# A one-core decoder block: the projections' weight sums on VectorE instead of GpSimd, and rotary units with five tiles and earlier loads

## The chip, the core and the metric

One Trainium2 chip, one core of it. A core has TensorE (PE in the rows: matmuls), VectorE (DVE), ScalarE (ACT), GpSimd (POOL) and SyncE (SP, which here only issues loads), with an on-chip memory (SBUF), eight accumulator banks (PSUM) and DMA queues to the memory of the chip. An engine works through its instructions in the order in which they stand in its queue; an instruction whose input is missing holds up all that stands behind it. The metric is the device time of one execution in microseconds. Three executions of the kernel before took 1737.4, 1739.75 and 1740.69 us; the median, 1739.75 us, is the time before.

## The reference, cut to what matters

A block of a decoder on 1024 tokens of 1024 features in float32: one wide projection of the normed input feeds a recurrent branch (LRU) and a dilated-window attention branch; gates merge the two; a SwiGLU feed-forward layer follows.

```python
h = rms_norm(x, pre_mix_norm)
xr, gr, q, k, v, gates = split(h @ w_in)            # the projections
xr = causal_depthwise_conv(xr, conv_w, conv_b)      # 4 taps
xr = rg_lru(xr, ...)                                # two gate matmuls, then a scan over time
y_lru = (xr * gelu(gr)) @ w_lru_proj
q, k = partial_rope(q, cos, sin) * HEAD_DIM ** -0.5, partial_rope(k, cos, sin)   # 32 of 128 features
y_attn = dilated_window_attention(q, k, v) @ w_attn_proj
x = x + rms_norm((g_lru * y_lru + g_attn * y_attn) @ w_out)     # g_*: sigmoid(gates)
x = x + rms_norm((silu(n @ w_ffn_gate) * (n @ w_ffn_up)) @ w_ffn_down)           # n: rms_norm(x)
```

## The kernel before

The program runs in stages: the v projection (to about 140 us), the other projections (to about 720), attention with the LRU's and attention's output projections (to about 950), `w_out`, the feed-forward products (1060 to 1510) and the down projection. All but the middle stages are made of **quads**. A quad is a 2 by 2 block product done in seven block products instead of eight (Strassen's scheme in Winograd's form): `P1, P2, P6, P5, P3, P7, P4`, in this order on PE. A float32 operand is split into a high and a low part (`split`, L98 and L99: ACT writes the high part `whi`, DVE subtracts and writes the low part `wlo`), and a product is three matmuls, high-high, low-high and high-low (L133 to L135), for each of four blocks of 128 rows: 12 matmuls of 128x512 to a product, each product into one PSUM bank `pq`.

The projections stage has 28 quads: 0 to 7 for `gr` and `xr` in turn, 8 to 19 for q and k (three attention groups of four heads), 20 to 27 for the gates `gl` and `ga`. `Quad.prep` prepares the weights of a quad while PE is in the quad before it. It loads two blocks `r0` and `r1` (tiles `wraw`, two buffers, both on SP's queue), forms four sums of 128x512 each on GpSimd (L267 to L270: the two halves of `sb` and of `sa`), and splits `r0` (for P1 and P2), `sa` (P6 and P7), `sb` (P5 and P3) and half of `r1` (`w4h`, `w4l`, one buffer, for P4). `sa` and `sb` have one buffer each. As `wraw` has two buffers, the load of a next `r1` waits until the last split of this one, `w4l`, has read it. In `body`, DVE adds the finished products to each other: `uw` (L309), and `fb` (L728, in `proj`), which GpSimd's queue stores (L734).

After every product `run_quads` calls `tick()`, which runs what `todo` has for that count (7 to a quad). There are two kinds of extra work:

- 16 LRU units, from tick 15 on, one every 8 ticks. `lru_a` loads 515 columns of `xr`, forms the convolution on DVE in four instructions (L776, and three times L778: `xc`) and splits it (`xch`, `xcl`); `lru_b`, four ticks later, has six gate matmuls (`pgt<-xch,gw` and `pgt<-xcl,gw`), then sigmoids on ACT, a product on GpSimd (L799), a product and the scan on DVE (L800, L803), and a second product on GpSimd (L807).
- 6 rotary units, ticks 148 to 173, one every 5 ticks. `rotate_load` loads four tiles of 256 KB (`rq1`, `rq2` from the stored q and k, `rcs` and `rsn` from a table `rtd`), five ticks ahead of `rotate`, which has six products or sums on DVE (L825 to L830) and two stores on GpSimd's queue (L833).

Both kinds take their tiles from one ring of `B2` = 10 buffers (tag `b2`), so a load waits for the last reader of a buffer ten tiles earlier. The order of the instructions on an engine isn't the code's alone: where the program is built, instructions that don't depend on each other can be exchanged, as L269 ahead of L268 in some quads. The feed-forward quads use the same class later.

Of the kernel before, what the change touches and what calls it, by code (L numbers as in the profile page):

```python
# [40 lines left out]
EARLYP = {6: (0,), 7: (1,)}  # L41
ORDER = [(s[0], int(s[1])) for s in "t6 h1 p2 p3 x5 h0 t7 x6 x4 h2 x7 h3".split()]
B4 = 19
B2 = 10
LRU0, LRUD = 15, 8
ROPE0, ROPED = 148, 5


V_CB, V_BR, V_BI, V_LAM, V_CW, V_GP, V_END = 0, 8, 16, 24, 32, 64, 72
# [13 lines left out]
def block(ctx, tc, a, out):  # L63
    nc = tc.nc
    V, A, G, T = nc.vector, nc.scalar, nc.gpsimd, nc.tensor
# [19 lines left out]
    def b4(name, dt=F32, shape=(128, 1024)):  # L85
        return bp.tile(list(shape), dt, name=name, tag="b4")
# [7 lines left out]
    def split(src, hi, lo, he=None, le=None):  # L94
        if he is G:
            G.tensor_scalar(hi, src, 1.0, 0.0, op0=OP.mult, op1=OP.add)
        else:
            A.activation(hi, src, AF.Copy)  # L98
        (le or V).tensor_sub(lo, src, f(hi))  # L99
# [132 lines left out]

    class Quad:
        pool = up = X = None
        P1B, W4 = 2, 1
        NAMES = dict(P1="b11", P2="b21", P6="t2", P7="t3", P5="t1", P3="b22", P4="t4")
        w = None
# [22 lines left out]
            self.unit(self.raw(0, name), ("P1", "P2"))  # L260

        def prep(self):
            r0, r1 = self.raw(0), self.raw(1)
            lo_, hi_ = slice(0, 512), slice(512, 1024)
            sa = Quad.pool.tile([128, 1024], F32, name="sa")
            sb = Quad.pool.tile([128, 1024], F32, name="sb")
            G.tensor_add(sb[:, lo_], r1[:, lo_], r1[:, hi_])  # L267
            G.tensor_sub(sa[:, lo_], sb[:, lo_], r0[:, lo_])  # L268
            G.tensor_sub(sa[:, hi_], r0[:, lo_], r1[:, lo_])  # L269
            G.tensor_sub(sb[:, hi_], r0[:, hi_], sa[:, lo_])  # L270
            if self.w is None:
                self.w = {}
                self.unit(r0, ("P1", "P2"))
            self.unit(sa, ("P6", "P7"))
            self.unit(sb, ("P5", "P3"))
            h4 = Quad.pool.tile([128, 512], F32R, name="w4h", bufs=Quad.W4)
            l4 = Quad.pool.tile([128, 512], F32R, name="w4l")
            split(r1[:, hi_], h4, l4)
            self.w["P4"] = h4, l4
# [47 lines left out]
    def run_quads(quads, pre, tick=None):  # L327
        quads[0].prep()
        for j in range(pre):
            quads[j].first()  # L330
        for j, q in enumerate(quads):
            if j + 1 < len(quads):
                quads[j + 1].prep()
            for _ in q.body():
                if tick:
                    tick()
            if pre <= j + 1 < len(quads):
                quads[j + 1].head()
                if tick:
                    tick()  # L340
                quads[j + 1].first()
                if tick:
                    tick()
# [92 lines left out]
    def rates(ss):  # L436

        s = sp.tile([128, 4], F32, name="rs4", bufs=2)
        last_act[0] = A.activation(s, ss, AF.Sqrt, bias=epsc, scale=1.0 / D)
        r = sp.tile([128, 4], F32, name="rr4", bufs=2)  # L440
        V.reciprocal(r, s)
        e = sp.tile([128, 4], F32, name="re4", bufs=2)
        V.scalar_tensor_tensor(e, ss, D * EPS, r, op0=OP.add, op1=OP.mult)
        V.scalar_tensor_tensor(e, e, 1.0 / D, r, op0=OP.mult, op1=OP.mult)
        V.scalar_tensor_tensor(e, e, -3.0, r, op0=OP.add, op1=OP.mult)
        V.tensor_scalar(r, e, -0.5, None, op0=OP.mult)
        dg = sp.tile([128, 4, 128], F32, name="dg")
        for t in range(4):
            last_dve[0] = V.tensor_scalar(dg[:, t], ident, e[:, t:t + 1], None, op0=OP.mult)
        rb = ps("prb")  # L450
        last_rb[0] = T.matmul(rb, ones, dg.rearrange("p t n -> p (t n)"), start=True, stop=True)
        return r, rb
# [65 lines left out]
    r0, rb = rates(ss[0])  # L518
# [13 lines left out]
    r1, rb = rates(ss[1])  # L532
# [222 lines left out]
    def b2(name, dt=F32, shape=(128, 512)):  # L755
        return lp.tile(list(shape), dt, name=name, tag="b2")
# [64 lines left out]
    def rotate(g, u):  # L821

        t1, t2, cs, sn = RT.pop((g, u))
        m1, m2 = b2("rm1"), b2("rm2")
        V.tensor_mul(m1, t2, sn)  # L825
        V.tensor_mul(m2, t1, sn)
        V.tensor_mul(t1, t1, cs)
        V.tensor_mul(t2, t2, cs)
        V.tensor_sub(t1, t1, m1)
        V.tensor_add(t2, t2, m2)  # L830
        c = slice(512 * u, 512 * u + 512)
        for i, t in enumerate((t1, t2)):
            G.dma_start(qkd[g, :, :, 16 * i:16 * i + 16, c].rearrange("h s p n -> (h s) p n"), t)  # L833
# [5 lines left out]
    todo = {1: [(late_rates, ())]}  # L839
# [3 lines left out]
        todo.setdefault(LRU0 + LRUD * n, []).append((lru_a, unit))  # L843
        todo.setdefault(LRU0 + LRUD * n + 4, []).append((lru_b, unit))
    for n in range(6):
        todo.setdefault(ROPE0 + ROPED * (n - 1), []).append((rotate_load, (n // 2, n % 2)))
        todo.setdefault(ROPE0 + ROPED * n, []).append((rotate, (n // 2, n % 2)))
    clock = [0]

    def tick():  # L850
        clock[0] += 1
        for fn, args in todo.pop(clock[0], ()):
            fn(*args)
# [9 lines left out]
    ap = actx.enter_context(tc.tile_pool(name="ap", bufs=2, reuse_waits="tile"))  # L863
    lp = lctx.enter_context(tc.tile_pool(name="lp", bufs=B2, reuse_waits="tile"))
    op1 = fctx.enter_context(tc.tile_pool(name="op1", bufs=1, side="right", reuse_waits="tile"))
# [224 lines left out]
    for n, (fn, args) in enumerate(EARLYA):  # L1090
        todo.setdefault(fn, []).append((after, args))
    run_quads(q1, PRE1, tick)
    assert not todo
    fctx.close()
# [65 lines left out]
    for nb in range(KT):  # L1160
        if nb % 2 == 0:
            w = wunit(a["w_ap"][nb // 2])
        mx, m1 = b4("mix"), b4("m1")
# [110 lines left out]
    quads = [q for i in range(NF // 2) for q in hidden(i)]  # L1274
# [58 lines left out]
    octx = ExitStack()  # L1333
    op = octx.enter_context(tc.tile_pool(name="op", bufs=1, side="right", reuse_waits="tile"))
    Quad.up = op
    run_quads(quads, PRE)


# [146 lines left out]
    def fetch(n):  # L1485
        if n < len(steps):
            ops[steps[n]] = operands(*steps[n])
# [117 lines left out]
```

## Time and profile before

| what | value |
|---|---|
| median of three executions | 1739.75 us |
| the profiled execution | 1737.8 us |
| its span from the first to the last instruction | 1736.0 us |
| PE busy | 1676.3 us, 97% of the span |
| DVE, ACT, POOL busy | 1121.0, 728.4, 693.2 us |

The profiled execution took 1737.8 us, of which 1.8 us lie outside the span. A busy PE isn't always PE at its full rate: at the lower of its two clocks a matmul takes longer and counts as busy all the same. So in the rows further down the number of matmuls in a stretch and the column PEclk (the clock that was granted, as a share of the full one) are read beside the busy time. The rows name an instruction by its line, engine, operation and `out<-in`; numbers of buffers are left out where they don't matter. In a list of waits the columns are the total time, the number of times and the longest time; in a timeline, start, length and, in brackets, the idle time of the engine ahead of the instruction with what ended it.

### The profile page before, as it was taken

The page shows a single profiled execution, that of the slowest core. Times are in us where ns is not written, and L with a number is a line of the kernel's source. Part 1 is how long each engine was busy: PE and PEld are TensorE (multiplying, and loading weights), DVE is VectorE, ACT ScalarE, POOL GpSimd, SP SyncE. Part 2 cuts the span into 40 slices and gives each one's busy share as a digit, 9 for nine tenths or more (in the row PEclk, how much of TensorE's full clock was granted, in tenths as well). Part 3 has the DMA queues.
Part 4 walks back from the last instruction along what each step waited for, and adds up shares of the span by engine and source line. Part 5 has one row for each costly group of instructions (what it writes and reads, how often), then busy time and mean ns, then how long its engine had stood idle before and what let it go on. Part 6 is the DMA issues. An engine that isn't in the chain of part 4 may idle for free.

```text
span 1736.0 us, 21088 instructions
## 1 busy us (share of the span) xinstructions
PE 1676.3 (97%) x7748; PEld 1376.8 (79%) x7748; DVE 1121.0 (65%) x1591; ACT 728.4 (42%) x1130; POOL 693.2 (40%) x644
## 2 busy tenths in 40 slices
PE   9999999999999999989999999799999999999996
PEld 7897888787877887868888787678888888788885
DVE  7956577778887766554433678755554555659658
ACT  6423367564555532564441445323222222345343
POOL 2003454554445533133334205576566666400103
PEclk9999999999999999999999999899999999999998
DMA  8233433343333564683519742133222222475353
GB/s 322 85 123 123 146 128 130 131 149 118 128 133 134 167 206 156 229 317 135 195 50 359 245 147 73 61 123 126 103 91 103 92 96 105 160 255 191 109 188 121
DMA packets 95919, 262.70 MB, mean 151 GB/s; under 512 B 13768, under 2 KB 22120, under 8 KB 94408
## 3 DMA queue, kind: packets, MB, share of 16 engines
q1 hardware_dynamic: 70352, 182.49, 31.2%
q0 software_dynamic: 20352, 76.21, 11.6%
q10 hardware_dynamic: 5112, 2.66, 0.5%
q8 instruction: 61, 1.00, 0.2%
q14 instruction: 42, 0.34, 0.1%
HBM read 180.86 MB, written 80.35 MB: 150 GB/s over the span
## 4 chain that ended last, share of the span: by engine, by line
PE 77%; DVE 10%; DMA 4%; issue 4%; POOL 3%; ACT 3%; SPq 0%; ACTq 0%; DVEq 0%; POOLq 0%
PE pq L135 15%; PE pq L134 15%; PE pq L133 15%; PE pd L1351 4%; PE pd L1352 4%; PE pd L1350 4%; PE py L135 2%; PE py L133 2%; PE py L134 2%; PE pv L463 2%; PE po L1033 2%; PE pv L134 1%; PE pv L135 1%; DMA rsn<-rtd 1%; PE pv L133 1%
## 5 line engine op out<-in xcount | busy, mean ns | idle before, releaser
L133 PE MATMUL pq<-hth,whi 128*128 128x512 f32 x448 | 179.3, 400 | 2.7 <-ACT whi L98 2.7
L135 PE MATMUL pq<-hth,wlo 128*128 128x512 f32 x448 | 178.5, 399 | 3.1 <-DVE wlo L99 3.1
L134 PE MATMUL pq<-htl,whi 128*128 128x512 f32 x448 | 180.5, 403 | 0.0
L267 POOL TENSOR_TENSOR sb<-wraw 128x512 f32<-128x512 f32 x50 | 70.9, 1418 | 168.3 <-DMA wraw<-in_w_fg 92.1
L98 ACT ACTIVATE whi<-sa 128x1024 fp32r<-128x1024 f32 x50 | 52.9, 1059 | 198.6 <-PE pq L134 139.4
L1351 PE MATMUL pd<-fbl,fah 128*128 128x512 f32 x304 | 119.6, 394 | 4.5 <-DVE fbl L99 4.5
L1352 PE MATMUL pd<-fbh,fal 128*128 128x512 f32 x304 | 119.7, 394 | 0.0
L1350 PE MATMUL pd<-fbh,fah 128*128 128x512 f32 x304 | 119.4, 393 | 0.0
L99 DVE TENSOR_TENSOR wlo<-wraw,whi 128x1024 fp32r<-128x1024 f32 x67 | 97.5, 1456 | 23.6 <-ACT whi L98 20.8
L98 ACT ACTIVATE whi<-wraw 128x1024 fp32r<-128x1024 f32 x67 | 70.7, 1056 | 90.8 <-PE pq L134 26.3
L309 DVE TENSOR_TENSOR uw<-pq,uw 128x512 f32<-128x512 f32 x100 | 68.4, 684 | 57.6 <-PE pq L135 56.8
L133 PEld LDWEIGHTS pq<-hth,whi 128*128 128x128 f32 x448 | 85.8, 191 | 24.7 <-ACT whi L98 3.2
L135 PEld LDWEIGHTS pq<-hth,wlo 128*128 128x128 f32 x448 | 85.5, 191 | 24.3 <-DVE wlo L99 3.8
L134 PEld LDWEIGHTS pq<-htl,whi 128*128 128x128 f32 x448 | 85.7, 191 | 20.3
L1424 POOL TENSOR_TENSOR y<-y,gpf 128x512 f32<-128x512 f32 x16 | 26.2, 1663 | 186.0 <-ACT fah L98 109.7
L99 DVE TENSOR_TENSOR wlo<-sa,whi 128x1024 fp32r<-128x1024 f32 x50 | 70.1, 1402 | 27.7 <-ACT whi L98 27.7
L728 DVE TENSOR_TENSOR fb<-pq,uw 128x512 f32<-128x512 f32 x84 | 67.8, 807 | 30.6 <-PE pq L135 30.3
L1256 POOL TENSOR_TENSOR fo<-fo,ut 128x512 f32<-128x512 f32 x44 | 60.6, 1381 | 66.4 <-DVE ut L1255 66.4
L98 ACT ACTIVATE fah<-ar 128x1024 fp32r<-128x1024 f32 (+1 forms) x41 | 40.8, 995 | 98.6 <-PE pd L1351 76.5
L99 DVE TENSOR_TENSOR fal<-ar,fah 128x1024 fp32r<-128x1024 f32 (+1 forms) x41 | 49.3, 1203 | 48.7 <-ACT fah L98 48.6
L268 POOL TENSOR_TENSOR sa<-sb,wraw 128x512 f32<-128x512 f32 x50 | 80.2, 1604 | 0.0
L133 PE MATMUL pq<-t1h,whi 128*128 128x512 f32 x200 | 79.4, 397 | 0.5 <-ACT whi L98 0.5
(541 smaller groups left out, 4946.9 us busy)
## 6 DMA issues: line engine op xcount, KB each, us to landing
ar<-fd SPq DMA_DIRECT2D x35, 512.0 KB
qkd<-fb POOLq DMA_DIRECT2D x24, 512.0 KB, 3.6
qk<-qkd SPq DMA_DIRECT2D x24, 512.0 KB
wraw<-in_w_fg SPq DMA_DIRECT2D x24, 512.0 KB
wraw<-in_w_fu SPq DMA_DIRECT2D x24, 512.0 KB
fd<-fo POOLq DMA_DIRECT2D x11, 1024.0 KB, 4.3
wd<-in_w_dn SPq DMA_DIRECT2D x21, 512.0 KB
fd<-fs POOLq DMA_DIRECT2D x11, 768.0 KB, 5.6
```

Source lines behind the costliest of these rows:

```text
L98: A.activation(hi, src, AF.Copy)
L99: (le or V).tensor_sub(lo, src, f(hi))
L133: T.matmul(o, lh, rh, start=(first and i == 0), stop=False)
L134: T.matmul(o, lh, rl, start=False, stop=False)
L135: T.matmul(o, ll, rh, start=False, stop=(last and i == n - 1))
L267: G.tensor_add(sb[:, lo_], r1[:, lo_], r1[:, hi_])
L268: G.tensor_sub(sa[:, lo_], sb[:, lo_], r0[:, lo_])
L309: V.tensor_add(y, bank, x)
L728: V.tensor_add(o, half_in(bank, g), half_in(add, g))
L1350: T.matmul(o, ah[:, ts], bh, start=(i == 0), stop=False)
L1351: T.matmul(o, ah[:, ts], bl, start=False, stop=False)
L1352: T.matmul(o, al[:, ts], bh, start=False, stop=(i == NP - 1))
```

## The change

The constants, `Quad` and `run_quads`:

```diff
-B2 = 10
+B2 = 11
-ROPE0, ROPED = 148, 5
+ROPE0, ROPED, ROPEL = 148, 5, 3
...
     class Quad:
+        sum_engine, SUMS = V, 1
...
         def prep(self):
-            r0, r1 = self.raw(0), self.raw(1)
+            self.fetch()
+            self.sums()
+
+        def fetch(self):
+            self.r = self.raw(0), self.raw(1)
+
+        def sums(self):
+            r0, r1 = self.r
             lo_, hi_ = slice(0, 512), slice(512, 1024)
+            G = Quad.sum_engine
+            if self.w is None:
+                self.w = {}
+                self.unit(r0, ("P1", "P2"))
             sa = Quad.pool.tile([128, 1024], F32, name="sa")
             sb = Quad.pool.tile([128, 1024], F32, name="sb")
             G.tensor_add(sb[:, lo_], r1[:, lo_], r1[:, hi_])
             G.tensor_sub(sa[:, lo_], sb[:, lo_], r0[:, lo_])
             G.tensor_sub(sa[:, hi_], r0[:, lo_], r1[:, lo_])
             G.tensor_sub(sb[:, hi_], r0[:, hi_], sa[:, lo_])
-            if self.w is None:
-                self.w = {}
-                self.unit(r0, ("P1", "P2"))
             self.unit(sa, ("P6", "P7"))
...
             if j + 1 < len(quads):
-                quads[j + 1].prep()
-            for _ in q.body():
+                quads[j + 1].fetch()
+                if Quad.SUMS < 0:
+                    quads[j + 1].sums()
+            for n, _ in enumerate(q.body()):
+                if j + 1 < len(quads) and n == Quad.SUMS:
+                    quads[j + 1].sums()
                 if tick:
                     tick()
```

The rotary units, and the line ahead of the feed-forward quads:

```diff
-        m1, m2 = b2("rm1"), b2("rm2")
+        m1 = b2("rm1")
         V.tensor_mul(m1, t2, sn)
-        V.tensor_mul(m2, t1, sn)
+        V.tensor_mul(sn, t1, sn)
         V.tensor_mul(t1, t1, cs)
         V.tensor_mul(t2, t2, cs)
         V.tensor_sub(t1, t1, m1)
-        V.tensor_add(t2, t2, m2)
+        V.tensor_add(t2, t2, sn)
...
-        todo.setdefault(ROPE0 + ROPED * (n - 1), []).append((rotate_load, (n // 2, n % 2)))
+        todo.setdefault(ROPE0 + ROPED * (n - 1) - ROPEL, []).append((rotate_load, (n // 2, n % 2)))
...
     Quad.up = op
+    Quad.sum_engine, Quad.SUMS = G, -1
     run_quads(quads, PRE)
```

In the projections the four sums of a quad are VectorE's now, and they, with all the splits of that quad, are written after the second product of `body`, P5, of the quad ahead; the two loads are still written ahead of `body`. The split of `r0` stands ahead of the sums in the code. The feed-forward quads keep the sums on GpSimd and ahead of `body`. A rotary unit takes five tiles of the ring, which has eleven buffers, and its loads are written eight ticks ahead of it.

On GpSimd 112 instructions are gone, L267 to L270 of 28 quads; nothing takes their place. On PE the order is the same but for one matmul of quad 0's preparation. On DVE, around one LRU unit (its input tile is `xr__3603`), stands before:

```order
L99 TENSOR_TENSOR wlo<-sb,whi 128x1024
L800 TENSOR_TENSOR it<-it,a__3528 128x512
L99 TENSOR_TENSOR w4l<-wraw,w4h 128x512
L803 SCALAR_TENSOR_TENSOR it<-at__3527,it 128x512
L728 TENSOR_TENSOR fb<-pq,uw 128x512
L806 COPY carry<-it 128x1
L99 TENSOR_TENSOR gw<-gwr,gw 128x256
L776 TENSOR_SCALAR xc<-xr__3603,vec 128x512
L778 SCALAR_TENSOR_TENSOR xc<-xr__3603,vec,xc 128x512 x3
L728 TENSOR_TENSOR fb<-pq,p_3646 128x512
L99 TENSOR_TENSOR wlo<-wraw,whi 128x1024
L99 TENSOR_TENSOR xcl<-xc,xch 128x512
```

In the changed kernel, from the same `w4l` on (L741, L789 and L791 are the lines that were L728, L776 and L778):

```order
L99 TENSOR_TENSOR w4l<-wraw,w4h 128x512
L819 COPY carry<-it 128x1
L741 TENSOR_TENSOR fb<-pq,uw 128x512
L99 TENSOR_TENSOR gw<-gwr,gw 128x256
L789 TENSOR_SCALAR xc<-xr__3603,vec 128x512
L791 SCALAR_TENSOR_TENSOR xc<-xr__3603,vec,xc 128x512 x3
L279 TENSOR_TENSOR sb<-wraw 128x512
L741 TENSOR_TENSOR fb<-pq,p_3646 128x512
L99 TENSOR_TENSOR wlo<-wraw,whi 128x1024
L99 TENSOR_TENSOR xcl<-xc,xch 128x512
L318 TENSOR_TENSOR uw<-pq,p_3646 128x512
L280 TENSOR_TENSOR sa<-sb,wraw 128x512
```

The first sum `sb<-wraw`, which reads the newly loaded `r1`, stands behind the convolution and ahead of `fb`, the split of `r0` and `xcl`. In other places nothing stands between it and the `w4l` that lets that load go. This is DVE's queue in the changed kernel where a later LRU unit, that of `xr__4583`, begins:

```order
L99 TENSOR_TENSOR w4l<-wraw,w4h 128x512
L279 TENSOR_TENSOR sb<-wraw 128x512
L281 TENSOR_TENSOR sa<-wraw 128x512
L741 TENSOR_TENSOR fb<-pq,p_4479 128x8x64
L99 TENSOR_TENSOR wlo<-wraw,whi 128x1024
L280 TENSOR_TENSOR sa<-sb,wraw 128x512
L282 TENSOR_TENSOR sb<-wraw,sa 128x512
L318 TENSOR_TENSOR uw<-pq,p_4479 128x512
L808 SCALAR_TENSOR_TENSOR a__4496<-a__4496,rt 128x512
L318 TENSOR_TENSOR uw<-pq,uw 128x512
L789 TENSOR_SCALAR xc<-xr__4583,vec 128x512
L791 SCALAR_TENSOR_TENSOR xc<-xr__4583,vec,xc 128x512
```

`w4l` is followed at once by the sum that reads the next load; before, only `fb` stood behind that `w4l`. At the rotary units (0 to 5) SP's queue has before, from unit 3's four loads to the first of unit 5:

```order
L109 DMA rq_5317<-qkd 128x1x512
L109 DMA rq_5318<-qkd 128x1x512
L109 DMA rcs<-rtd 128x1x512
L109 DMA rsn<-rtd 128x1x512
L109 DMA wraw<-in_w_g 128x1024 x2
L109 DMA rq_5427<-qkd 128x1x512
L109 DMA rq_5428<-qkd 128x1x512
L109 DMA rcs<-rtd 128x1x512
L109 DMA rsn<-rtd 128x1x512
L109 DMA wraw<-in_w_g 128x1024 x2
L109 DMA rq_5550<-qkd 128x1x512
```

and in the changed kernel, between the same loads:

```order
L109 DMA rq_5243<-qkd 128x1x512
L109 DMA rq_5244<-qkd 128x1x512
L109 DMA rcs<-rtd 128x1x512
L109 DMA rsn<-rtd 128x1x512
L109 DMA wraw<-in_w_g 128x1024 x2
L109 DMA rq_5345<-qkd 128x1x512
L109 DMA rq_5346<-qkd 128x1x512
L109 DMA rcs<-rtd 128x1x512
L109 DMA rsn<-rtd 128x1x512
L109 DMA rq_5476<-qkd 128x1x512
```

Between the loads of units 4 and 5 no weight loads stand any more; unit 5's have moved ahead of a pair of them. On DVE the last unit's first product has moved up with them:

```order
L99 TENSOR_TENSOR wlo<-sa,whi 128x1024
L838 TENSOR_TENSOR rm_5544<-rq_5346,rsn 128x512
L838 TENSOR_TENSOR rm_5634<-rq_5477,rsn 128x512
L741 TENSOR_TENSOR fb<-pq,uw 128x512
L99 TENSOR_TENSOR wlo<-sb,whi 128x1024
```

The splits are those of quad 24. `rm_5634` belongs to unit 5 and stands ahead of an `fb` and of the split of `sb`; before, unit 5's first product stood behind the quad's last split, `w4l`, and the next split of an `r0`.

## Rows read from the trace of the kernel before

**Rows 1.** Page, part 1: busy time of each engine (share of the span)

```profile
PE 1676.3 (97%) x7748; PEld 1376.8 (79%) x7748; DVE 1121.0 (65%) x1591; ACT 728.4 (42%) x1130; POOL 693.2 (40%) x644
```

**Rows 2.** Stretches of 50 us: busy us (instructions), clock, DMA

```profile
core 0: us, PE busy (x) PEld busy (x) DVE busy (x) ACT busy (x) POOL busy (x), PEclk, DMA share, GB/s
150.00:200.00 50.00, 46.81 (x190) 36.83 (x189) 28.93 (x31) 16.48 (x21) 22.85 (x20) 0.93 0.37 123
200.00:250.00 50.00, 50.00 (x216) 40.34 (x216) 35.12 (x51) 34.99 (x44) 21.28 (x18) 1.00 0.36 125
...
300.00:350.00 50.00, 48.51 (x206) 38.12 (x205) 41.19 (x48) 24.82 (x31) 27.82 (x21) 1.00 0.39 129
...
400.00:450.00 50.00, 46.29 (x188) 36.71 (x187) 37.92 (x43) 26.19 (x32) 19.93 (x17) 0.93 0.35 126
...
500.00:550.00 50.00, 49.78 (x213) 39.67 (x212) 43.00 (x50) 27.82 (x34) 20.57 (x19) 1.00 0.36 125
550.00:600.00 50.00, 48.15 (x200) 38.20 (x199) 40.85 (x52) 30.70 (x38) 25.59 (x21) 0.97 0.49 163
600.00:650.00 50.00, 50.00 (x217) 40.27 (x216) 28.81 (x41) 14.38 (x20) 22.70 (x24) 1.00 0.62 199
650.00:700.00 50.00, 46.86 (x195) 37.30 (x194) 31.00 (x43) 16.09 (x24) 15.79 (x18) 0.97 0.50 161
```

**Rows 3.** What PE waited for, 140 to 720: total us, times, longest

```profile
PE pgt L133 <- ACT xch L98: 3.9, 3, 2.2
PE pgt L134 <- DVE xcl L99: 3.4, 5, 1.5
PE pq L133 <- ACT whi L98: 3.2, 2, 2.7
PE pq L135 <- DVE wlo L99: 3.1, 1, 3.1
```

**Rows 4.** POOL's groups, 150 to 720: busy us, mean ns | idle before, releasers

```profile
L269 POOL TENSOR_TENSOR sa<-wraw 128x512 f32<-128x512 f32 x28 | 43.4, 1552 | 0.5 <-DMA rtd<-rot 0.4
...
L267 POOL TENSOR_TENSOR sb<-wraw 128x512 f32<-128x512 f32 x28 | 41.4, 1477 | 75.7 <-DMA wraw<-in_w_k 34.2 <-DMA wraw<-in_w_g 20.5 <-DMA wraw<-in_w_xr 13.8
```

**Rows 5.** DVE's groups in the same stretch

```profile
L99 DVE TENSOR_TENSOR wlo<-wraw,whi 128x1024 fp32r<-128x1024 f32 x26 | 37.8, 1454 | 1.6 <-ACT whi L98 1.4
...
L99 DVE TENSOR_TENSOR wlo<-sb,whi 128x1024 fp32r<-128x1024 f32 x28 | 34.1, 1217 | 1.3 <-ACT whi L98 1.2
...
L99 DVE TENSOR_TENSOR xcl<-xc,xch 128x512 fp32r<-128x512 f32 x16 | 15.6, 972 | 4.3 <-ACT xch L98 4.2
L778 DVE SCALAR_TENSOR_TENSOR xc<-xr__3603,vec,xc 128x512 f32<-128x512 f32 x3 | 8.2, 2749 | 0.1
...
L826 DVE TENSOR_TENSOR rm<-rq,rsn 128x512 f32<-128x512 f32 x6 | 4.1, 681 | 0.0
...
L778 DVE SCALAR_TENSOR_TENSOR xc<-xr__3408,vec,xc 128x512 f32<-128x512 f32 x3 | 2.2, 744 | 0.0
```

**Rows 6.** Timeline near 151: start, length, instruction, idle before it

```profile
150.59 1.09 ACT L294 ACTIVATE p<-pq 128x512 f32<-128x512 f32 x2 [5.11 <-DMA rtd<-rot]
...
153.03 1.06 ACT L98 ACTIVATE whi<-sa 128x1024 fp32r<-128x1024 f32 x1 [0.84 <-POOL sa L268]
```

**Rows 7.** Timeline of SP's queue, POOL, DVE and PE, 417 to 430

```profile
417.04 0.33 SPq L109 DMA_DIRECT2D wraw<-in_w_k  x1
...
421.36 1.30 POOL L267 TENSOR_TENSOR sb<-wraw 128x512 f32<-128x512 f32 x1
...
428.25 1.05 DVE L728 TENSOR_TENSOR fb<-pq,p 128x512 f32<-128x512 f32 x1
...
429.11 0.50 PE L133 MATMUL pgt<-xch,gw 128*128 128x512 f32 x1 [2.23 <-ACT xch L98]
```

**Rows 8.** Timeline of DVE near 546

```profile
546.65 0.69 DVE L800 TENSOR_TENSOR it<-it,a__4496 128x512 f32<-128x512 f32 x1 [2.70 <-POOL it L799]
```

**Rows 9.** Timeline of SP's queue and DVE, 643 to 655

```profile
643.09 0.58 SPq L109 DMA_DIRECT2D rsn<-rtd  x1
...
654.49 0.69 DVE L825 TENSOR_TENSOR rm<-rq,rsn 128x512 f32<-128x512 f32 x1 [9.81 <-DMA rsn<-rtd]
```

## The prediction

> **What bounds the kernel now.** The page's busy times come first: PE is busy for 1676.3 of 1736.0 us, no other engine for over 1121.0 [rows 1]. So a change pays only where PE stands or runs slowly. The change touches the projections alone, so the second view is PE by stretches of 50 us over that stage [rows 2]. An undisturbed stretch has 50.00 us of busy PE, clock 1.00 and 216 or 217 matmuls (there are five such, 200:250 and 600:650 among them, 216.6 on average), that is 0.2308 us for each. The number of matmuls that is missing from the other stretches, times 0.2308, is what PE lost there, standing and slow clock together:
>
> - 150:200: 190 matmuls, 26.6 missing, 6.1 us (A);
> - 300:350: 206, 10.6 missing, 2.4 us (B);
> - 400:450: 188, 28.6 missing, 6.6 us (D);
> - 500:550: 213, 3.6 missing, 0.8 us (F);
> - 550:600: 200, 16.6 missing, 3.8 us (E);
> - 650:700: 195, 21.6 missing, 5.0 us (G).
>
> The sum is 24.7 us, and this is the most that the change can win. PE's list of waits for the stage names who was late [rows 3]: 3.9 + 3.4 us for `xch` and `xcl` (the gate matmuls of the LRU units: B, D, E, F), 3.2 us for `whi` (A), 3.1 us for `wlo` (G), 13.6 us in all. The remaining 11 us are slow clock: in A, D, E and G, where PE stood longest, the mean clock is 0.93 to 0.97, in B and F it stays at 1.00 [rows 2]. So a shorter stop, below some 1 us, costs only itself, and a longer one about doubles.
>
> Who made them late? In D the three convolution instructions of one unit took 2749 ns each; another unit's took 744 [rows 5]. They ran while GpSimd went through the sums that begin at 421.36, and PE, free since 426.9, waited 2.23 us for `xch` alone [rows 7]. In E, DVE stood 2.70 us for GpSimd's product `it`, which was queued behind sums [rows 8]. In G, DVE stood 9.81 us for the table `rsn` of a rotary unit, whose load was issued at 643.09 and came at 654.49 [rows 9], with the split of `sa` queued behind. In A, ACT stood 5.11 us, `p` came at 150.59, and `whi` waited for GpSimd's sum `sa` until 153.03 [rows 6].
>
> **The sums on VectorE.** Removed from GpSimd: 112 instructions, 28 to each line, of 1477 and 1552 ns on the average in the two shown [rows 4], some 160 us, all beside PE's work. Added to DVE: 112 of 128x512 with two SBUF inputs; such an instruction takes 681 ns with GpSimd idle [rows 5], so 112 x 0.68 = 76 us. Given back: what sums on GpSimd stretched on DVE. The 26 splits `wlo<-wraw` have 1454 ns against 1217 of `wlo<-sb`, 6.2 us; the 16 `xcl` 972 against 681, 4.7 us; D's unit alone 3 x 2.0 = 6.0 us [rows 5]. Over all kinds of instructions I estimate 40 us (at least these 17, at most the 76 at which DVE's load would not change). DVE's load in the fullest stretch, 43.0 of 50 [rows 2], thus gets 2.5 quads x 4 x 0.68 = 6.8 more and loses about 4: 46 of 50. Its cover is thin, but it does not overflow.
>
> Against the change speaks a rule of the Trainium skill ("Perfetto Trace Analysis", "Optimizing Scalar/DVE Operations"): a saturated DVE is to be relieved by giving work to ScalarE or even GpSimd; the same paragraph adds that offloading between GpSimd and DVE may not help, since they share an SBUF read port. By the first half the fullest stretch would reach 49.8 of 50 and the second rival below would be the outcome; by the second half it stays near 46. The 2749 ns against 744 above speak for the second half.
>
> What it does at each place:
> - D: convolution at 420.01 + 3 x 0.74 = 422.2 instead of 428.25. Behind it now stand the first sum, `fb` (1.05 us, [rows 7]), `wlo` 1.22 and `xcl` 0.68. The load that the sum waits for was issued at 417.04 and had landed at 421.36 [rows 7], before DVE comes to it. So `xcl` ends near 422.2 + 0.7 + 1.1 + 1.2 + 0.7 = 425.9, and PE is free at 426.9. Saved: all of 6.6 us, with a margin of 1 us.
> - E: the 2.70 us and the stretched instructions go, two sums and their wait come in. I take 2.8 of 3.8 us.
> - B and F: their stops are short and made by the same stretching; the sums put about as much in front of `xcl`. I take 1.0 of 3.2 us.
> - A: one sum on DVE is 0.6 us shorter than on GpSimd (1.29 us at 421.36 against 0.68), but two of them follow `w4l` or `p` as before, and `p` itself still comes at 150.59. I take 1.5 of 6.1 us, since the stop stays above 1 us and so does its slow clock.
>
> **The new wait.** The first sum stands in DVE's queue, and reads `r1`, whose load can begin only when the last `w4l` has been read. From issue to landing this took 4.3 us [rows 7]; GpSimd stood 75.7 us for such loads over 28 quads [rows 4], 2.7 us each. Where nothing stands between `w4l` and the sum, DVE now stands for up to 4.3 us, and behind it wait `fb`, the split of `r0` and, in some units, the convolution and `xcl`. A `uw` or `fb` that is 4 us late costs nothing while PE has banks left, and the splits of the next quad are several products ahead. Only the gate matmuls are tight: `lru_b` follows `lru_a` by four products. For 16 units I allow two new stops of 1 to 1.5 us without slow clock: 3 us (bounds: none, and several with slow clock, in the rival).
>
> **The rotary part.** It adds no instruction; per unit one buffer less. The loads are written 3 products earlier, at 12 matmuls x 0.2308 = 2.8 us each 8.3 us. G's load took 11.4 us to come [rows 9]; issued 8.3 us earlier it comes about when it is wanted, and the 3.14 us at PE go. In the ring of eleven, unit 5's loads wait for unit 3's tiles, and its first product now stands ahead of an `fb` and of quad 24's split of `sb`. Unit 3 is run one and a half quads ahead of that split's use, so the loads should go out near 646 and land by 657 at the latest; PE needs the split at about 660. I take 4.5 of 5.0 us. SP's queue: weight loads pushed back behind waiting rotary loads (a pair, by some 4 us) are wanted a quad later, so nothing.
>
> **Sum.** 6.6 + 2.8 + 1.0 + 1.5 + 4.5 = 16.4 won, 3 lost: -13.4. Against the profiled execution's 1737.8 us this gives 1724.4; the median of the runs lies 1.95 higher, at 1739.75, and with it the forecast is 1726. Nothing else moves: the later stages keep their instructions, and begin earlier.
>
> **The rivals.**
> 1. All of it goes: every stop of the stage, A's too: 1739.75 - 24.7 = 1715. For it speaks that GpSimd's queue is near empty after the change; against it A, whose `p` waits for a DMA, not for a sum.
> 2. The wait on `r1` at the head of DVE's queue makes gate matmuls late with the slow clock. The price is D's, 6.6 us for one. The 16.4 us are given back after 2.5 such units; four take it to -16.4 + 26.4 = +10, 1750, three to +3.4, 1743. It needs DVE to stand 4.3 us where my margin is 1 us. For it: DVE at 43.0 of 50 already, and the sum directly behind `w4l` in the stretch of E. Against it: the stretching, which made the longest stops, goes with the sums.
> 3. The rotary stop only moves: unit 5's tiles come after 660 and hold the split of `sb`. G's 4.5 us stay and the gain is 8.9: 1731. For it: the 11.4 us that such a load took, and that it waits for stores and products of unit 3.
> 4. The change does not do what it says: GpSimd keeps two products per LRU unit, and DVE is stretched by these as before. Then D's and E's gains halve and new stops take the rest: -3, 1737, within the noise.
>
> **How the numbers follow.** Forecast (1721 to 1730) 0.47, first rival 0.10, third 0.15, fourth or a mix of stops that evens out 0.13, second 0.15. The likeliest gives 1726. Leaving out half of the second rival gives an upper end of 1744, and the lower end, 1715, is the first rival's. Within 0.2% (3.5 us, about what a measurement of this kernel can tell from no change) is "same": 1736.3 to 1743.2. Faster 0.72, same 0.13, slower 0.15.
>
> **What would show it.** In the profile after: at D the convolution at 0.75 us an instruction and no wait for `xch`; 400:450 and 650:700 with 216 matmuls at clock 1.00; sums at 0.69 us on DVE, with 1 to 4 us of waiting for `wraw` in front of the first; DVE busier by about 36 us over the stage; 150:200 still with a stop. I am wrong if gate matmuls wait for `xch` or `xcl` by over 7 us in all, as before, or if PE waits at all for the split of `sb` in quad 24.

## The result, and the profile after

The changed kernel takes 1720.26 us (median of four runs, 1717.53 to 1720.78) against 1738.58 us for the kernel before in four runs: ratio 0.9897, 95% interval 0.9876 to 0.9918, that is 18 us less. The forecast was 13.4 us less. The span of the profiled execution fell by the same, from 1736.0 to 1718.0 us.

PE by stretches of 50 us, the changed kernel (columns as in [rows 2], whose rows these answer to):

```profile
150.00:200.00 50.00, 47.54 (x198) 37.69 (x197) 34.88 (x50) 16.93 (x22) 2.22 (x4) 0.97 0.39 132
...
300.00:350.00 50.00, 50.00 (x217) 40.33 (x216) 43.78 (x65) 27.81 (x35) 12.72 (x13) 1.00 0.40 138
...
400.00:450.00 50.00, 50.00 (x216) 40.32 (x215) 43.69 (x61) 27.83 (x34) 9.32 (x11) 1.00 0.37 133
...
500.00:550.00 50.00, 48.72 (x209) 38.77 (x208) 42.72 (x55) 27.41 (x36) 12.09 (x12) 1.00 0.39 144
550.00:600.00 50.00, 50.00 (x217) 40.29 (x216) 44.33 (x63) 26.89 (x33) 11.55 (x13) 1.00 0.55 185
600.00:650.00 50.00, 50.00 (x216) 40.30 (x215) 35.48 (x53) 15.41 (x22) 5.42 (x9) 1.00 0.59 192
650.00:700.00 50.00, 50.00 (x217) 40.29 (x216) 37.01 (x53) 19.56 (x27) 5.88 (x11) 1.00 0.58 187
sum 550.00, PE 546.26 PEld 439.19 DVE 439.91 ACT 287.01 POOL 99.42; mean PE 49.66 PEld 39.93 DVE 39.99 ACT 26.09 POOL 9.04
```

Two stretches are still short of 216.6 matmuls. With 0.2308 us for each missing one, A still loses 18.6 x 0.2308 = 4.3 us and 500:550 loses 1.75; all others are full. Lost in the stage: 6.0 us instead of 24.7. The 18.7 us between them make the 18.0 by which the spans differ; in the rest of the program 0.7 us went the other way, and the largest change there is PE's wait for a load of q and k where attention starts, 3.2 us before and 5.4 after. What PE waited for from 140 to 720 us, in the same columns as [rows 3]:

```profile
PE pq L133 <- ACT whi L98: 2.5, 2, 1.7
PE pgt L134 <- DVE xcl L99: 1.1, 1, 1.1
PE pgt L133 <- ACT xch L98: 0.2, 1, 0.2
```

The gate matmuls wait 1.3 us in all instead of 7.3, and nothing waits for `wlo`. At D (it answers to [rows 7]) the timeline of the changed kernel has, on DVE and on PE:

```profile
417.41 2.33 DVE L791 SCALAR_TENSOR_TENSOR xc<-xr__3603,vec,xc 128x512 f32<-128x512 f32 x3
419.65 0.68 DVE L279 TENSOR_TENSOR sb<-wraw 128x512 f32<-128x512 f32 x1
420.25 1.06 DVE L741 TENSOR_TENSOR fb<-pq,p 128x512 f32<-128x512 f32 x1
421.23 1.22 DVE L99 TENSOR_TENSOR wlo<-wraw,whi 128x1024 fp32r<-128x1024 f32 x1
422.37 0.68 DVE L99 TENSOR_TENSOR xcl<-xc,xch 128x512 fp32r<-128x512 f32 x1
...
423.78 0.40 PE L133 MATMUL pgt<-xch,gw 128*128 128x512 f32 x1
```

The convolution's three instructions take 2.33 us together instead of 8.32, the sum doesn't wait, and `xcl` is done at 423.05, 0.7 us ahead of the first gate matmul. DVE's groups show what the sums cost there (busy us, mean ns | idle before):

```profile
L279 DVE TENSOR_TENSOR sb<-wraw 128x512 f32<-128x512 f32 x27 | 20.2, 748 | 48.4 <-DMA wraw<-in_w_g 19.2 <-DMA wraw<-in_w_k 16.8 <-DMA wraw<-in_w_gr 6.5
...
L99 DVE TENSOR_TENSOR xcl<-xc,xch 128x512 fp32r<-128x512 f32 x16 | 10.9, 683 | 0.8 <-ACT xch L98 0.7
```

DVE stands 48.4 us for the loads at the head of its queue, and no gate matmul waits for it except in one unit. `xcl` is back at 683 ns from 972 [rows 5]. Over the stage DVE is busy for 439.91 us; before, the eleven stretches add up to 402.61:

```profile
sum 550.00, PE 536.39 PEld 428.45 DVE 402.61 ACT 279.64 POOL 255.88; mean PE 48.76 PEld 38.95 DVE 36.60 ACT 25.42 POOL 23.26
```

The rotary part, on DVE (it answers to [rows 9]):

```profile
637.84 0.69 DVE L838 TENSOR_TENSOR rm<-rq,rsn 128x512 f32<-128x512 f32 x1
644.23 0.69 DVE L838 TENSOR_TENSOR rm<-rq,rsn 128x512 f32<-128x512 f32 x1 [5.71 <-DMA qkd<-rq]
644.84 0.68 DVE L741 TENSOR_TENSOR fb<-pq,uw 128x512 f32<-128x512 f32 x1
645.44 1.21 DVE L99 TENSOR_TENSOR wlo<-sb,whi 128x1024 fp32r<-128x1024 f32 x1
```

DVE still stands, 5.71 us, at unit 5's first product. It waits for a store of unit 3 now, whose tile the product overwrites. But behind it stand only an `fb` and the split of `sb`, and the split comes in time.

### The profile page after: what moved, and what is told of

The parts are those of the page before. It is cut to its first block, busy times and chain, and to the rows that moved or that the text cites. A ratio compares the mean times of both kernels' runs of the same rounds, so it can differ in the third digit from the quotient of the medians.

```text
span 1718.0 us, 21008 instructions
## 1 busy us (share of the span) xinstructions
PE 1667.8 (97%) x7748; PEld 1373.4 (80%) x7748; DVE 1148.9 (67%) x1703; ACT 729.3 (42%) x1130; POOL 528.4 (31%) x532
## 4 chain that ended last, share of the span: by engine, by line
PE 58%; DVE 6%; DMA 3%; ACT 1%; issue 1%; POOL 1%; ACTq 0%; SPq 0%; DVEq 0%; POOLq 0%
PE pq L135 11%; PE pq L134 11%; PE pq L133 10%; PE pd L1365 4%; PE pd L1366 4%; PE pd L1364 4%; PE py L135 2%; PE py L134 2%; PE py L133 2%; PE po L1046 2%; PE pe L135 1%; PE pe L133 1%; PE pe L134 1%; PE ppt L1034 1%; DMA wraw<-in_w_ap 1%
## 5 line engine op out<-in xcount | busy, mean ns | idle before, releaser
L99 DVE TENSOR_TENSOR wlo<-wraw,whi 128x1024 fp32r<-128x1024 f32 x67 | 92.1, 1376 | 21.3 <-ACT whi L98 18.5
L741 DVE TENSOR_TENSOR fb<-pq,uw 128x512 f32<-128x512 f32 x84 | 67.8, 808 | 25.5 <-PE pq L135 25.1
L99 DVE TENSOR_TENSOR wlo<-sa,whi 128x1024 fp32r<-128x1024 f32 x50 | 69.3, 1387 | 20.9 <-ACT whi L98 20.9
L134 PE MATMUL pq<-t1l,whi 128*128 128x512 f32 x200 | 79.0, 395 | 0.0
L134 PE MATMUL pq<-t3l,whi 128*128 128x512 f32 x200 | 78.7, 394 | 0.0
```

The costliest lines, as they stand in the source:

```text
L134: T.matmul(o, lh, rl, start=False, stop=False)
L741: V.tensor_add(o, half_in(bank, g), half_in(add, g))
```

## The experiments

All runs are compared with runs of the kernel before on the same chip. Since the times of one kernel spread over some 5 us, the place of a gain is read from the trace: the "loss in the stage" of the table is the number of matmuls missing from the eleven stretches of 150 to 700 us, times 0.2308, as in the prediction. It is read from one execution, and two of the changed kernel have 6.0 and 8.4, so a difference of 2 us in it says little. Where the stop A begins ahead of 150 us, its first part isn't counted: 0.8 us with the loads five ahead, 0.6 with the ring of ten. Each number under "matmuls" is a stretch that is not full, with its start.

| kernel | matmuls in the stretches that aren't full | loss in the stage, us | median, us | ratio to before, interval |
|---|---|---|---|---|
| before | [rows 2] | 24.7 | 1738.58 | 1 |
| rotary part alone | 150: 189, 300: 206, 400: 188, 500: 213, 550: 199 | 20.3 | 1731.93 | 0.9971, 0.9960 to 0.9982 |
| sums alone | 150: 197, 500: 209, 600: 192, 650: 211 | 13.2 | 1721.55 | 0.9916, 0.9886 to 0.9945 |
| GpSimd, moved | 150: 188, 300: 208, 450: 213, 500: 205 | 12.1 | 1723.80 | 0.9926, 0.9903 to 0.9950 |
| VectorE, early | 150: 203, 300: 205, 450: 208, 500: 215 | 8.2 | 1721.51 | 0.9911, 0.9885 to 0.9937 |
| changed | 150: 198, 500: 209 | 6.0 | 1720.26 | 0.9897, 0.9876 to 0.9918 |
| one quad | 150: 192, 300: 205, 450: 214, 500: 204, 550: 211, 650: 183 | 20.9 | 1728.70 | 0.9956, 0.9942 to 0.9970 |
| gate products too | 150: 197, 500: 196 | 9.3 | 1720.37 | 0.9902, 0.9883 to 0.9922 |
| loads five ahead | 150: 206, 500: 208, 600: 193 | 9.9 | 1720.81 | 0.9915, 0.9891 to 0.9940 |
| ring of ten | 150: 205, 500: 199, 600: 211 | 8.0 | 1719.11 | 0.9896, 0.9876 to 0.9916 |
| tables on two queues | 150: 207, 300: 214, 500: 208 | 4.8 | 1718.12 | 0.9887, 0.9863 to 0.9910 |
| the same again | 150: 208, 500: 208 | 4.0 | 1719.41 | 0.9896, 0.9877 to 0.9914 |
| changed again | 150: 196, 500: 201 | 8.4 | 1721.29 | 0.9907, 0.9890 to 0.9925 |
| tables, sums after P3 | 150: 208, 300: 215, 500: 199 | 6.4 | 1716.57 | 0.9882, 0.9867 to 0.9897 |

**Sums alone, and rotary part alone.** The first is the changed kernel with the rotary lines as before:

```diff
-B2 = 11
+B2 = 10
-ROPE0, ROPED, ROPEL = 148, 5, 3
+ROPE0, ROPED, ROPEL = 148, 5, 0
-        m1 = b2("rm1")
+        m1, m2 = b2("rm1"), b2("rm2")
-        V.tensor_mul(sn, t1, sn)
+        V.tensor_mul(m2, t1, sn)
-        V.tensor_add(t2, t2, sn)
+        V.tensor_add(t2, t2, m2)
```

> The changed kernel with the rotary units as before (ten buffers in the ring, six tiles to a unit, loads five products ahead); only the sums are on VectorE and written after P5. Theory (the sums' engine does most of it, and the rotary part is a term of its own): the stop of PE before the split of sa in quad 24 (3.1 us and its slow clock, 5.0 us in all) comes back, the stops at the gate matmuls stay away: 1725 us, between 1723 and 1728, ratio to before 0.992. Rival (the rotary loads are what mattered, by their traffic or by DVE's standing): 1734 or more.

The second is the kernel before with these lines the other way round.

> The kernel before with the rotary part of the change alone (eleven buffers, five tiles, loads eight products ahead); the sums stay on GpSimd and where they were. Theory: only the stop at quad 24 goes: 1738.6 - 5.0 = 1733.6 us, between 1732 and 1736, ratio 0.997. Rival of the rotary loads: 1725 or less.

Sums alone: 1721.55. Its one stop for a split in quad 24:

```profile
PE pq L135 <- DVE wlo L99: 3.8, 1, 3.8
```

That stop and its slow clock cost 24.6 + 5.6 missing matmuls in 600:700, 7.0 us, more than the 5.0 of G. Rotary part alone: 1731.93, and 650:700 is full, while D is what it was:

```profile
400.00:450.00 50.00, 46.29 (x188) 36.66 (x187) 37.68 (x43) 26.27 (x32) 19.46 (x17) 0.93 0.36 129
...
650.00:700.00 50.00, 50.00 (x216) 40.28 (x215) 31.56 (x42) 18.90 (x26) 19.45 (x20) 1.00 0.50 160
```

So the two parts are apart from each other: the rotary part takes G away, the sums all but one stop of what the gates lost. The second expectation held; the sums alone did somewhat better than the 1723 to 1728 expected, with the stop that was named.

**GpSimd, moved, and VectorE, early.** The change of the sums is two changes, the engine and the place in the code. Two runs separate them; both have the rotary part.

```diff
-        sum_engine, SUMS = V, 1
+        sum_engine, SUMS = G, 1
```

> The changed kernel with the sums back on GpSimd, but written after P5 as in the changed kernel, the rotary part as changed. This sets the engine apart from the place. Theory (the engine: GpSimd's sums stretch VectorE's instructions and hold up GpSimd's own queue): the convolution instructions of some units take 1.7 us and more again instead of 0.75, gate matmuls wait some 7 us in all and the time comes to 1733 us, between 1729 and 1738. Rival (the place: sums and splits written later leave VectorE and ScalarE free for the gates): 1720 to 1723, no wait of the gates over 1.5 us.

```diff
-        sum_engine, SUMS = V, 1
+        sum_engine, SUMS = V, -1
```

> The changed kernel with the sums on VectorE but written ahead of body, where they stood before, instead of after P5; the rotary part as changed. Theory of the engine: 1720 us within 3 us, since the order on VectorE follows mostly from when the loads come, not from where the sums are written. Rival (the place): the first sum waits for its load at the head of VectorE's queue earlier and longer, gate matmuls wait over 5 us in all, 1728 or more.

Here the theory missed. With the sums left on GpSimd and only written later, the time is 1723.80 where 1733 was expected, and the loss in the stage falls from the 20.3 of the rotary part alone to 12.1. D is gone. Its timeline, on DVE and POOL:

```profile
420.86 2.33 DVE L791 SCALAR_TENSOR_TENSOR xc<-xr__3603,vec,xc 128x512 f32<-128x512 f32 x3
...
425.34 1.77 DVE L99 TENSOR_TENSOR xcl<-xc,xch 128x512 fp32r<-128x512 f32 x1
...
422.54 1.80 POOL L279 TENSOR_TENSOR sb<-wraw 128x512 f32<-128x512 f32 x1 [1.03 <-DMA wraw<-in_w_k]
```

The sums still stretch what runs beside them: `xcl` takes 1.77 us. But in this order `w4l` stands behind the scan on DVE, so the load that it lets go comes later, and the first sum begins at 422.54 when the convolution is nearly through. Before, it began at 421.36, and GpSimd went on beside it with hardly a gap. Where the two meet, PE still stops: this kernel has gate stops of 1.8 us at 309 and of 1.0 and 1.0 us at 548. With the sums on VectorE but written early, the time is within the 3 us of 1720 that were expected, and the loss is 8.2 us, with gate stops of 0.6, 1.5 and 1.4 us at 304, 329 and 498. Without A, which the clock also moves, the gate stops cost 13.9 us with the rotary part alone, 5.5 with the place, 5.0 with the engine and 1.75 with both. So each half alone takes 8 to 9 us of them away, and both together 12: no difference between the engine and the place is shown. Both runs also have the split of `r0` written ahead of the sums, which no run takes back.

**One quad.** If D is a meeting of four sums with one convolution, moving those four alone must end it. In the kernel before, quad 14 alone has its sums on VectorE:

```diff
+        eng = G
...
-            G.tensor_add(sb[:, lo_], r1[:, lo_], r1[:, hi_])
+            E = self.eng
+            E.tensor_add(sb[:, lo_], r1[:, lo_], r1[:, hi_])
...
+    q1[14].eng = V
```

> The kernel before with the four sums of a single quad, number 14, on VectorE (those that run at 421 to 427 us beside the convolution of xr__3603); the other 27 quads keep theirs on GpSimd, nothing else is changed. Theory (the longest gate stop, D, is made by these four sums running beside one convolution): the three convolution instructions take 0.75 us each instead of 2.75, PE's waits of 2.2 and 1.5 us at that unit go with their slow clock, and the time falls by 6.6 us, to 1731 or 1732; the stops at 331, at 554 and in quad 24 stay. Rival (GpSimd's queue and the order of the splits make the stop): the stop stays or only moves by a unit, gain under 2 us.

```profile
400.00:450.00 50.00, 50.00 (x217) 40.28 (x216) 41.57 (x53) 26.32 (x32) 21.50 (x17) 1.00 0.36 126
650.00:700.00 50.00, 45.00 (x183) 35.80 (x182) 32.44 (x45) 18.21 (x26) 17.01 (x19) 0.93 0.49 158
```

400:450 is full at clock 1.00, with four instructions moved out of 112: D's 6.6 us were this meeting. Two of the three convolution instructions take 0.75 us; the first, beside GpSimd's product of the unit before, still takes 1.97. The time fell to 1728.70, ratio 0.9956, in line with the 6.6 expected. The profiled execution, 1734.44 us, is the slowest of the ten: G came out worse in it (5.0 us of waiting), which shows how little the size of one stop is fixed.

**Gate products too.** GpSimd's two products for each LRU unit also go to VectorE:

```diff
-        G.tensor_mul(i, i, w["xc"])
+        V.tensor_mul(i, i, w["xc"])
...
-        G.tensor_mul(i, i, gel)
+        V.tensor_mul(i, i, gel)
```

> The changed kernel with the two products that each LRU unit still has on GpSimd moved to VectorE too (32 instructions). Theory (what is left of the stretching makes the last gate stop, at 543 us, where one convolution instruction takes 1.77 us beside the product with gel): that stop of 1.3 us goes, 1719 us, 0 to 2 us below the changed kernel. Rival (VectorE is near its limit and 32 x 0.69 = 22 us more are too much): new gate stops, 1724 or more.

The time is the changed kernel's, 1720.37, and the last gate stop grew, from 1.3 to 2.8 us:

```profile
PE pgt L133 <- ACT xch L98: 1.7, 1, 1.7
PE pgt L134 <- DVE xcl L99: 1.1, 1, 1.1
```

So that stop isn't what is left of the stretching. In the changed kernel one convolution instruction did take 1.77 us there, but in this run, where all three take 0.73 to 0.75 us, the third starts no earlier: on DVE it stands behind the scan, two splits and now a gate product.

```profile
538.18 0.73 DVE L791 SCALAR_TENSOR_TENSOR xc<-xr__4583,vec,xc 128x512 f32<-128x512 f32 x1
538.83 0.15 DVE L819 COPY carry<-it 128x1 f32<-128x1 f32 x1
538.89 1.22 DVE L99 TENSOR_TENSOR wlo<-sb,whi 128x1024 fp32r<-128x1024 f32 x1
540.02 0.69 DVE L820 TENSOR_TENSOR it<-it,gel__4481 128x512 f32<-128x512 f32 x1
540.63 0.75 DVE L791 SCALAR_TENSOR_TENSOR xc<-xr__4583,vec,xc 128x512 f32<-128x512 f32 x1
```

DVE works here without a gap from the first sum of the quad, which starts at 525.99 after 4.74 us of waiting for its load, up to `xcl`. It is what stands in DVE's queue behind that load, the four sums among it, that makes `xcl` late. This expectation missed.

**Loads five ahead, and ring of ten.** The rotary part is three edits; two runs take back one each.

```diff
-ROPE0, ROPED, ROPEL = 148, 5, 3
+ROPE0, ROPED, ROPEL = 148, 5, 0
```

> The changed kernel with the rotary loads five products ahead, as before; five tiles to a unit and eleven buffers stay. It separates the earlier issue from the ring. Theory (the earlier issue): DVE stands for a table again, PE stops at quad 24 for 3 us or more, 1725 us. Rival (one tile less and one buffer more already let the loads go early enough): 1720 to 1721, no stop at quad 24.

```diff
-B2 = 11
+B2 = 10
```

> The changed kernel with the ring at ten buffers instead of eleven; five tiles to a rotary unit and loads eight products ahead stay. Theory (the earlier issue does it, the eleventh buffer is not needed): no stop at quad 24, within 1 us of the changed kernel. Rival (the loads wait for buffers, and only the eleventh lets them go): a stop before the split of sa or sb in quad 24 of 2 to 4 us and its clock, 3 to 5 us more.

With the loads issued as before, PE waits 3.6 us for `wlo` in quad 24 again (5.4 us of loss in 600:650). With ten buffers it waits 1.0 us there (1.3 us of loss). The two lines, in this order:

```profile
PE pq L135 <- DVE wlo L99: 3.6, 1, 3.6
PE pq L135 <- DVE wlo L99: 1.0, 1, 1.0
```

So the earlier issue takes most of G away and the eleventh buffer the last microsecond. The medians, 1720.81 and 1719.11, don't show it, and the 1725 expected of the first was a miss: in its profiled execution the clock held at A (206 matmuls in 150:200 instead of 198), which gave about 1.1 us back there (8 x 0.2308, less the 0.8 us of the stop that lies ahead of 150). And in the v projection, which no edit here touches, 50:100 has 375 matmuls at clock 1.00 instead of 349 at 0.93. At clock 1.00 some 88 of these smaller matmuls fit into 10 us there, so that is 3 us more. A difference of a few us between kernels is within the spread of their runs.

**Tables on two queues.** A is what is left. `p` and the sum `sa` wait until the rotary tables, whose tiles they reuse, have been stored; GpSimd issues the six stores one behind another. Three go to SyncE:

```diff
-                G.dma_start(rtd[g, s].rearrange("f (b n) -> b f n", b=8), src[:, 128 * g:128 * g + 128])
+                (G if s else nc.sync).dma_start(rtd[g, s].rearrange("f (b n) -> b f n", b=8), src[:, 128 * g:128 * g + 128])
```

> The changed kernel with three of the six stores of the rotary tables issued by SyncE instead of all six by GpSimd. In the changed kernel PE stands 1.7 and 0.7 us at the first quad's end, because p and the sum sa wait until these stores have read their tiles; they are issued one behind another, 0.6 us each. Theory (the issuing sets it): the stores land some 1.8 us earlier, the stop shrinks to under 1 us and the clock holds: 2 to 4 us below the changed kernel, 1717. Rival (the transfer or ScalarE's sines set it): no change, 1720.

> The changed kernel with three of the six table stores issued by SyncE, once more beside the changed kernel. In its first run the stop at the first quad's end fell from 2.5 to 1.5 us and the clock held, but the wait for a load of q and k at the attention's start grew from 5.4 to 6.8 us. Theory (the later wait takes part of it back): 1 to 2.5 us below the changed kernel. Rival (all that is won is taken back): the same time within 0.5 us.

> The changed kernel itself once more, as the base for the three runs beside it on this chip. Ratio to the kernel before 0.988 to 0.992.

The wait for `whi` fell from 2.5 to 1.5 and 1.3 us in the two runs, the clock held, and 150:200 rose to 207 and 208 matmuls. Beside the changed kernel on one chip it is 1719.41 against 1721.29, 1.9 us less, as the second expectation had it, but with intervals that overlap; the stop stayed above the 1 us of the first. Where attention starts, PE waits for a load of q and k: 5.4 us in the changed kernel and 6.8 in the first of these runs, but 5.7 in the second and in the changed kernel beside it. So a loss there, on which the second expectation built, isn't shown.

**Tables, sums after P3.** The last run adds a later place for the sums to this.

```diff
-        sum_engine, SUMS = V, 1
+        sum_engine, SUMS = V, 2
```

> The changed kernel with the tables on two queues and the sums on VectorE written one product later, after P3. With the sums written ahead of body the gates waited 3.5 us in all, after P5 1.3 us. Theory (a later place lets the order on VectorE favour the convolution, and the splits have room): the stop at 543 us goes or shrinks and the time is within 2 us of the run with the tables on two queues. Rival (the sums come too late for P6 of the next quad): PE waits for whi or wlo of sa in several quads, 1725 or more.

1716.57 us is the shortest median of all, 4.7 us below the changed kernel on the same chip (ratios 0.9882 and 0.9907, intervals that just overlap). The expected reason isn't it: the stop at 541 us grew to 1.9 us, and the loss in the stage is 6.4 us, 2 us less than that of the changed kernel beside it and 2.4 us more than that of the tables alone. 1.5 us come from a shorter wait at attention's start (4.2 instead of 5.7). Over 1 us more lies in the v projection, which the edit doesn't touch: 363 matmuls in 50:100, against 353 in the changed kernel beside it and 350 with the tables alone. The rest stays open.

## Why the prediction was right, and where it was not

**D, 6.6 us, all won.** Right in the time and in the order that was worked out: `xcl` behind the sum, `fb` and `wlo`, with a forecast margin of 1 us; the row shows 0.7. The one-quad run shows the cause. What the prediction left out is that moving the sums in the code would have ended D by itself.

**E and F, 2.8 of 3.8 us expected of E.** Before, E and F lost 4.6 us; after, the one stop that is left, at the same unit, costs 1.75, so 2.85 were won. The 2.70 us that DVE stood for GpSimd's product are gone. The stop that stays was put to the sums and their wait, and the trace bears that out, as told below under the new wait.

**B, sized too low.** 1.0 of 3.2 us was expected for B and F; B alone gave its 2.4.

**A, 1.5 of 6.1 us expected, 1.8 won.** `p` still waits for the tables, as forecast, and the sums on DVE took 0.7 us out of the two stops (3.2 to 2.5 us); the rest is clock. In the run with the loads five ahead the clock held at A with stops of 2.6 us, so the reason given, that a stop above 1 us keeps its slow clock, doesn't hold in every execution.

**G, 4.5 of 5.0 us expected, 5.0 won.** By the earlier issue, as the run with the loads five ahead shows. Unit 5's first product does stand in front of the split of `sb`, for 5.71 us, and the split still comes in time; the third rival wasn't far.

**The new wait, 3 us lost expected: one stop found, and it costs 1.75.** DVE stood 48.4 us for its loads, 1.7 us a quad, where 2.7 was read off GpSimd. One gate stop lies behind such a wait, the one left of E. In the changed kernel, on DVE and PE:

```profile
526.77 0.69 DVE L279 TENSOR_TENSOR sb<-wraw 128x512 f32<-128x512 f32 x1 [4.71 <-DMA wraw<-in_w_k]
...
543.72 0.68 DVE L99 TENSOR_TENSOR xcl<-xc,xch 128x512 fp32r<-128x512 f32 x1
...
544.45 0.50 PE L134 MATMUL pgt<-xcl,gw 128*128 128x512 f32 x1 [1.07 <-DVE xcl L99]
```

Between the first two lines DVE has no gap of over 0.1 us. All nine profiles with the sums on VectorE and behind P5 or P3 look like this: a wait of 4.6 to 5.0 us at this sum, `xcl` 16.9 to 17.0 us behind it, and gate stops of 1.0 to 2.8 us. In four of the nine, the changed kernel's repeat among them, the clock fell as well and 500:550 lost 3.6 to 4.75 us. So the second rival had its ground here, at one unit where it needed 2.5. Whether the unit would stop without the wait isn't shown: with the sums on GpSimd and moved it stops too, 2.0 us, after DVE has stood 2.72 us for GpSimd's product.

At the other units the wait cost PE nothing. A part of it stands in for others: DVE's idle time in front of `uw` on PE fell by 24.7 us, before and after:

```profile
DVE uw L309 <- PE pq L135: 34.6, 18, 3.9
DVE uw L318 <- PE pq L135: 9.9, 9, 1.9
```

That is half of the 48.4. The wait that ends at 358.4 (4.91 us) was not made up soon: DVE had no gap of over 0.3 us for 22 us behind it, and still no gate matmul waited.

With B this is the term that was mis-sized: for B, E, F and the new stops together 1.0 + 2.8 - 3 = 0.8 us were expected, and 5.3 were won (7.0 lost before, 1.75 after). That is 4.5 of the 5.3 us between 13.4 and 18.7.

**The slow clock's share, and the rest of the program.** The prediction put all that PE lost beyond its waits, 11 us, down to the slow clock. In B and F PE stood 1.49 and 0.22 us [rows 2] and lost 2.4 and 0.8 with the clock at 1.00, so some 1.5 us of it had another cause. "Nothing else moves" wasn't so either: the wait where attention starts grew from 3.2 to 5.4 us.

**DVE's load.** 76 us were to come and about 40 to go; DVE's busy time rose by 439.91 - 402.61 = 37.3 us. In the fullest stretch before, 500:550, it is 42.72 of 50 where it was 43.0 and 46 was forecast; the fullest after is 550:600, with 44.33. The rule of the Trainium skill that was weighed ("Perfetto Trace Analysis", "Optimizing Scalar/DVE Operations") would by its first half, as the prediction priced it, have had 49.8 there; the trace agrees with the second half, that giving work from DVE to GpSimd might not help, as they share a read port.

**Which reason was too strong.** The text put the gate stops down to GpSimd's engine alone. The sums on GpSimd do stretch DVE's instructions, by rows before and in the run with the place moved. But a stretched instruction stops PE only where the convolution of a unit and the sums of a quad fall together, and the order of a few instructions on DVE decides that as well as the engine does.

## What to carry to other kernels

Before an engine's busy share is taken as a reason against moving work onto it, see how much of that share is made by the work that would move: here 76 us of new work raised VectorE's busy time by 37. A wait at the head of an in-order queue costs where something tight stands behind it and the engine has no gap in between: here 48 us of such waits had one late gate matmul behind them. Follow the queue from each wait to its next gap; the lengths alone don't tell. Where a stop comes from two streams that meet, look at when each starts: shifting one by a microsecond can be worth as much as moving it to another engine.

## What the runs showed of the hardware

One DVE instruction with two SBUF inputs can be held up through several GpSimd instructions, not only made slower by one: at D two convolution instructions took 3.21 and 4.28 us where 0.75 is usual (the prediction's 2749 ns is their mean with the third one, 0.75). GpSimd had five instructions in that time, one nearly behind the other (the second is in [rows 7]). In the trace of the kernel before:

```profile
420.01 8.32 DVE L778 SCALAR_TENSOR_TENSOR xc<-xr__3603,vec,xc 128x512 f32<-128x512 f32 x3
...
420.12 1.29 POOL L807 TENSOR_TENSOR it<-it,gel__3513 128x512 f32<-128x512 f32 x1
...
423.20 1.31 POOL L268 TENSOR_TENSOR sa<-sb,wraw 128x512 f32<-128x512 f32 x1
424.45 1.30 POOL L269 TENSOR_TENSOR sa<-wraw 128x512 f32<-128x512 f32 x1
425.69 1.29 POOL L270 TENSOR_TENSOR sb<-wraw,sa 128x512 f32<-128x512 f32 x1
```

The GpSimd instructions took 1.29 to 1.31 us each there, less than their mean of 1.48 and 1.55 us [rows 4]; the one on DVE waited. The Trainium skill ("GPSIMD Engine Reference", "Key points") names the contention with DVE instructions that have two SBUF inputs, since GpSimd shares VectorE's SBUF interfaces; the trace agrees, and adds that it can cost 3.5 us for one instruction.

A stop of the same length doesn't always cost the clock. At A the changed kernel's two stops are 2.5 us in all and the clock falls; with the loads five ahead they are 2.6 us and it holds. Both kernels from 150 to 160 us, the changed one first:

```profile
150.00:160.00 10.00, 7.54 (x26) 5.45 (x25) 6.07 (x9) 5.52 (x7) 0.00 (x0) 0.83 0.34 118
```

```profile
150.00:160.00 10.00, 8.18 (x34) 6.33 (x35) 9.27 (x14) 5.06 (x6) 0.00 (x0) 1.00 0.29 105
```

26 matmuls against 34. The second stretch leaves out the first 0.8 us of its stop, so the lower of the two clock levels (1.2 instead of 2.4 GHz) cost about 1.1 us of the 1.8. The same happens in the v projection, from 50 to 100 us, where PE stood 3.0 us both times; the changed kernel first, then the one with ten buffers:

```profile
50.00:100.00 50.00, 47.04 (x349) 45.64 (x348) 42.07 (x43) 20.31 (x23) 3.76 (x5) 0.93 0.42 147
```

```profile
50.00:100.00 50.00, 47.03 (x375) 45.58 (x374) 44.81 (x47) 20.35 (x23) 3.82 (x6) 1.00 0.46 158
```

At the last gate stop the clock held after 1.3 us of waiting in the changed kernel and fell after 1.6 in its repeat (granted 0.74 from 545 to 550). The prediction's rule of thumb, that a stop of over 1 us about doubles, holds for D and A before, less for G (3.1 us of waiting, 5.0 lost), and not for every stop of 2.5 us. What decides it wasn't found.
